# The down projections of a macaron SwiGLU computed by seven block products instead of eight, on one Trainium2 core

## The chip, the core and the metric

The kernel runs on one core of a Trainium2 chip. A core has TensorE (PE in the profile: matrix products, results in eight PSUM banks), VectorE (DVE) and ScalarE (ACT) for elementwise work, GpSimd (POOL), and a queue of transfers that SyncE (SP) issues. The metric is device microseconds (us) of one execution, median over runs. Before the change it is 2217.27 us (three runs, 2216.33 to 2218.95).

## What is computed

Two layers over 512 positions of width 1024. Each is

```
x = x + 0.5 * swiglu(rms_norm(x, ffn1_norm), ffn1_w_gate, ffn1_w_up, ffn1_w_down)
x = x + mix(rms_norm(x, mix_norm))              # two convolutions and a sparse attention, one output projection
x = x + cross_attention(rms_norm(x, xa_norm), rms_norm(mem, mem_norm))
x = x + 0.5 * swiglu(rms_norm(x, ffn2_norm), ffn2_w_gate, ffn2_w_up, ffn2_w_down)

swiglu(h, wg, wu, wd) = (silu(h @ wg) * (h @ wu)) @ wd        # 1024 -> 2816 -> 1024, float32
```

There are so four SwiGLU blocks, called FFN 1 to 4 here. The change is inside them.

## The kernel before

Everything is kept transposed: a chunk is 128 channels on the partitions by 512 positions. x has 8 chunks, the hidden layer 22. A product in float32 is made of three faster ones (`mm3`): each operand is split into a high part, which ACT rounds off (`whi`, or a slot `s`), and a low part, which DVE gets by subtraction (`wlo`), and hi\*hi, hi\*lo and lo\*hi are summed in PSUM. The split of every weight tile therefore costs one ACT and one DVE instruction, and needs one of NW = 4 buffers each for `whi` and `wlo`, which come free when PE has read them. Weights arrive in four staging buffers `stg` of 128x1024.

An FFN goes through the hidden layer in three parts (PARTS: 8, 8 and 6 chunks). In each part it first makes the hidden chunks (gate and up), then adds the part's share of the down product to x.

Gate and up: the first four hidden chunks (PLAIN) by ordinary products of 512 columns, the rest by a scheme with seven block products (Winograd's form of Strassen's). A pair of output chunks times a pair of position halves is a 2x2 block product; instead of eight half-sized products per 2x2 block it takes seven, named A to G, each of 128x128 weights by 256 positions, nf/2 steps j deep. For that, `load_sevens` forms four sums of weight quarters on DVE, and `sevens` forms four sums of input halves, once per FFN. `seven` sends the products to three PSUM banks: A is copied out by ACT, B is added to it by DVE, and so on; the last product G follows behind the A of the next call (the list `late`), since its bank has to be read first.

Down: ordinary products. For each of the 8 output chunks, nf steps of three 512-column matmuls, then one DVE instruction that adds half of the sum to x. In the last part each finished chunk of x is prepared for the next stage (`Norm.chunk`: a square on ACT, a POOL addition, a split on ACT and DVE).

What sets the order: all instructions are recorded first (`Plan.record`), given a cost (`price`) and due time, and then put in order for each engine by a list scheduler (`order`) that has the number of buffers and 62 slots (NSLOT) of 128x512. Each engine then works strictly in that order. The source line of every recorded operation is the same in the profile (L353), so groups are told apart by tile names.

Of the kernel before, what the change touches and what calls it, by code (L numbers as in the profile page):

```python
# [16 lines left out]
P = 128  # L17
# [56 lines left out]
def _quarters(c0, c1):  # L74
    return [(k, DC // 2, m, P, 2) for c in range(c0, c1, 2 * P) for m in (c, c + P) for k in range(2)]
# [95 lines left out]
class Plan:  # L171
# [30 lines left out]
    def record(self, eng, name, args, kw):  # L202
        op = Op()
        op.n, op.eng, op.name, op.args, op.kw, op.succ, op.est, op.floor = (
            len(self.ops), eng, name, args, kw, [], 0.0, self.floor)
        outs = [v for v in (args[0] if args else None, kw.get("out"), kw.get("accum_out")) if isinstance(v, View)]
        ins = [v for v in (*args[1:], *(v for k, v in kw.items() if k not in ("out", "accum_out")))
               if isinstance(v, View)]
        self.price(op, ins, outs)
        op.lat = self.SEEN[eng]  # L210
        deps = set()
# [24 lines left out]
        self.ops.append(op)  # L236

    def price(self, op, ins, outs):
# [27 lines left out]
    def order(self):  # L266
# [40 lines left out]
        while len(done) < len(self.ops):  # L307
# [15 lines left out]
            if op.name == "dma_start":  # L323
                bus = max(bus, t + 1.7) + op.way
                op.end = bus + 0.9
                lanes = lanes[1:] + [op.end + 1.0]
            else:
                op.end = t + cost
# [28 lines left out]
def trunk_kernel(ctx: ExitStack, tc: tile.TileContext, a: dict, out: bass.AP):  # L357
# [169 lines left out]
    def half_quarters(w, c0, m):  # L527
# [3 lines left out]
        for b0, bk, bc, bn, step in BLOCKS[name]:  # L531
            if step == 2 and b0 == 0 and bc == c0 + m * P:
# [3 lines left out]
    def load_sevens(w, c0):  # L536


        H = T
        top, low, s23, s4 = (planned(wpool, g, 1024, F32) for g in ("stg", "stg", "sum", "sum"))  # L540
        nc.sync.dma_start(top, half_quarters(w, c0, 0))
        nc.sync.dma_start(low, half_quarters(w, c0, 1))
        s4 = s4[:, :H]
        nc.vector.tensor_sub(s23[:, H:], top[:, :H], low[:, :H])
        nc.vector.tensor_add(low[:, :H], low[:, :H], low[:, H:])
        nc.vector.tensor_sub(s23[:, :H], low[:, :H], top[:, :H])
        nc.vector.tensor_sub(s4, top[:, H:], s23[:, :H])
        r = {}
        for t, names in ((top, "AB"), (low, "EG"), (s23, "FD"), (s4, "C")):
            hl = split(t, *(planned(wpool, g, 1024, F32R)[:, :t.shape[-1]] for g in ("whi", "wlo")))  # L550
            for i, name in enumerate(names):
                r[name] = [tuple(x[:, i * H + j * P:i * H + (j + 1) * P] for x in hl) for j in range(4)]
        return r

    def load_cols(w, c0, n=256, k0=0, nk=DC):
        return [load(w, k0, nk, c, min(P, c0 + n - c)) for c in range(c0, c0 + n, P)]

# [7 lines left out]
    def sevens(norm):  # L565


        H = T // 2
        r = {name: [] for name in "ABCDEFG"}
        first = None  # L570
        for j in range(DC // 2):
            xe, xo = slot(), slot()
            for i, x in enumerate((xe, xo)):
                c = 2 * j + i
                nc.vector.scalar_tensor_tensor(x, X[c], pcol(norm.gain, norm.i * DC + c), norm.rb, op0=ALU.mult,
                                               op1=ALU.mult)
            t12, t34 = slot(), slot()
            nc.vector.tensor_sub(t12[:, :H], xe[:, H:], xe[:, :H])
            nc.vector.tensor_sub(t12[:, H:], xo[:, H:], t12[:, :H])
            nc.vector.tensor_sub(t34[:, :H], xo[:, H:], xe[:, H:])  # L580
            nc.vector.tensor_sub(t34[:, H:], xo[:, :H], t12[:, H:])
            if j % 2 == 0:
                first = slot(F32R), slot(F32R)
            x = slice(j % 2 * H, (j % 2 + 1) * H)
            r["A"].append(split(xe[:, :H], first[0][:, x], first[1][:, x]))
            for t, names in ((xo, "BC"), (t12, "EF"), (t34, "DG")):
                hl = split(t)
                for i, name in enumerate(names):
                    r[name].append(tuple(y[:, i * H:(i + 1) * H] for y in hl))
        return r  # L590

    def ffn(l, which, norm, nxt, begin=None, end=None):
        wg, wu, wd = ((f"{which}_w_{n}", l) for n in ("gate", "up", "down"))
        H = T // 2
        late = []

        def seven(w, c0, x):


            ws = load_sevens(w, c0)  # L600
            u, v, q = (bank()[:, :H] for _ in range(3))
            o = slot(), slot()
            one, two = slot(), slot()

            def product(acc, name, start, stop):
                for j in range(DC // 2):
                    mm3(acc, ws[name][j], x[name][j], start and j == 0, stop and j == DC // 2 - 1,
                        skip_group_check=True)

            product(u, "A", True, True)  # L610
# [3 lines left out]
            product(v, "E", True, True)  # L614
            nc.scalar.activation(two[:, :H], v, AF.Copy)
            product(q, "B", True, True)
            nc.vector.tensor_add(o[0][:, :H], q, one[:, :H])
            product(u, "F", False, True)
            nc.scalar.activation(one[:, H:], u, AF.Copy)
            product(v, "C", False, True)  # L620
            nc.vector.tensor_add(o[0][:, H:], v, one[:, H:])
            product(u, "D", False, True)
            nc.vector.tensor_add(o[1][:, H:], u, two[:, :H])
            late.append(lambda: product(u, "G", False, True))
            return o, u

        for f0, nf in PARTS:
            hid = []
            last = f0 + nf == FC

            def gated(pg, pu):
# [6 lines left out]
                hid.append(split(g))  # L638

            def gated_sevens(g, u):  # L640
                (ga, gb), gq = g
                (ua, ub), uq = u
                for x in (slice(0, H), slice(H, T)):
                    nc.scalar.activation(ga[:, x], ga[:, x], AF.Silu)
                nc.vector.tensor_mul(ua, ua, ga)
                hid.append(split(ua))
                nc.scalar.activation(gb[:, H:], gb[:, H:], AF.Silu)
                nc.scalar.activation(gb[:, :H], gq, AF.Silu)
                nc.vector.tensor_mul(ub[:, H:], ub[:, H:], gb[:, H:])
                nc.vector.tensor_mul(ub[:, :H], uq, gb[:, :H])  # L650
                hid.append(split(ub))

            if begin and f0 == 0:
                begin(wg, wu)
                norm.finish()
                x7 = sevens(norm)
                for ob in opening:
                    gated(*ob)
            for b in range(1 if begin and f0 == 0 else 0, nf // 2):
                c0 = (f0 + 2 * b) * P  # L660
                if f0 == 0 and b < PLAIN:
                    wgt = load_cols(wg, c0)
                    wut = load_cols(wu, c0)
                    for i in range(2):
# [4 lines left out]
                        if b == 0 and i == 0:  # L669
                            norm.finish()  # L670
                            x7 = sevens(norm)
                        gated(pg, pu)
                else:
                    pair = [seven(w, c0, x7) for w in (wg, wu)]
                    late.append(lambda pair=pair: gated_sevens(*pair))
            while late:
                late.pop(0)()
            for mp in range(DC // 2):
                ws = load_cols(wd, mp * 256, 256, f0, nf)
                halves = end and last and mp == DC // 2 - 1  # L680
                for x in (slice(0, T // 2), slice(T // 2, T)) if halves else (slice(0, T),):
                    for i in range(2):
                        m = 2 * mp + i
                        o = bank()[:, x]
                        for k in range(nf):
                            mm3(o, part(ws[i], k), tuple(t[:, x] for t in hid[k]), k == 0, k == nf - 1)
                        nc.vector.scalar_tensor_tensor(X[m][:, x], o, 0.5, X[m][:, x], op0=ALU.mult, op1=ALU.add)
                        if last:
                            nxt.chunk(m, x)
                        if halves and x.start and i == 0:  # L690
                            end(0)
                if halves:
                    end(1)
# [46 lines left out]
    def mem_part(c):  # L740
        t = slot()
        nc.sync.dma_start(t, a["mem"][:, c * T:(c + 1) * T])
        return t
# [508 lines left out]
```

## Time and profile before

| | |
|---|---|
| median of three runs | 2217.27 us |
| the profiled execution, and its span | 2217.13 us, 2215.3 us |
| PE, DVE, ACT, POOL busy | 2183.5, 1675.1, 1063.5, 153.1 us |
| matmuls | 12922 |
| DMA, mean | 104 GB/s |
| granted TensorE clock, mean | 0.994 of full |

The span is what the profile covers; 1.8 us of the execution lie around it. PE's busy time is modelled, so a share near 100% says that PE always had a matmul under way, not that no faster order exists. Durations of neighbouring DVE instructions overlap a little, and the busy time of an engine counts an overlap once. A row of busy times by stretch reads: start:end, length, then busy us (instructions) of PE, its weight loads, DVE, ACT and POOL, then the granted clock's share, the DMA share and GB/s. A row in order of time reads: start us, duration us, engine, line, operation, output from inputs, shape, count, and in brackets the idle time before it and what ended it.

### The profile page before, as it was taken

To read this page: it belongs to the slowest core of one execution; us is meant where nothing else is said; L and a number is where in the kernel's file an instruction comes from. 1 tells how busy PE (TensorE), PEld (TensorE's weight loads), DVE (VectorE), ACT (ScalarE), POOL (GpSimd) and SP (SyncE) were. 2 spreads that over 40 slices of the span, in tenths; PEclk is the share of its full clock that TensorE was granted. 3 is DMA by queue.
4 is the path that set the end of the run, shared out by engine and by line. 5 is a ranking of instruction groups with operands and counts; after the bars stand their busy time and mean duration, and the time that the engine had idled before them with its cause. 6 is when DMAs were issued, how large, how long until landed. Compare 5 with 4: busy or idle time off the path is not lost. (4 is left out here: it accounts for less than half of the span.)

```text
span 2215.3 us, 32854 instructions
## 1 busy us (share of the span) xinstructions
PE 2183.5 (99%) x12922; PEld 1928.6 (87%) x12922; DVE 1675.1 (76%) x2748; ACT 1063.5 (48%) x1772; POOL 153.1 (7%) x111
## 2 busy tenths in 40 slices
PE   8999999998999999999999999999999999999998
PEld 7989897887788888999989998978787888989897
DVE  8958578999965496766687685779998556958585
ACT  5536255325944353544544453532377344525353
POOL 3000002101020200000100000020100102000001
PEclk9999999999999999999999999999999999999999
DMA  6333333445332223343324333343543313233322
GB/s 216 99 92 113 97 88 110 127 113 145 97 113 67 84 80 113 87 124 86 108 84 121 89 111 90 101 135 89 142 126 104 96 44 99 86 98 113 114 80 74
DMA packets 83755, 230.09 MB, mean 104 GB/s; under 512 B 9616, under 2 KB 23056, under 8 KB 83600
## 3 DMA queue, kind: packets, MB, share of 16 engines
q1 hardware_dynamic: 83600, 228.00, 35.5%
q8 instruction: 101, 1.65, 0.3%
q14 instruction: 54, 0.44, 0.1%
HBM read 211.70 MB, written 2.10 MB: 97 GB/s over the span
## 5 line engine op out<-in xcount | busy, mean ns | idle before, releaser
L353 PE MATMUL ps<-s,whi 128*128 128x256 f32 (+2 forms) x7608 | 1770.4, 330 | 0.8 <-DVE s L353 0.8
L353 PEld LDWEIGHTS ps<-s,whi 128*128 128x128 f32 (+1 forms) x7608 | 1265.0, 190 | 137.1 <-issue 4.3
L353 PE MATMUL ps<-s,wlo 128*128 128x256 f32 (+2 forms) x3804 | 1176.0, 330 | 0.5 <-DVE wlo L353 0.5
L353 PEld LDWEIGHTS ps<-s,wlo 128*128 128x128 f32 (+1 forms) x3804 | 693.6, 190 | 64.7 <-DVE wlo L353 0.7
L353 ACT ACTIVATE whi<-stg 128x1024 fp32r<-128x1024 f32 (+1 forms) x398 | 413.1, 1042 | 694.1 <-PE ps L353 481.0
L353 DVE TENSOR_TENSOR wlo<-stg,whi 128x1024 fp32r<-128x1024 f32 (+1 forms) x398 | 476.0, 1197 | 102.7 <-ACT whi L353 102.3
L353 DVE TENSOR_TENSOR s<-ps,s 128x256 f32<-128x256 f32 (+2 forms) x372 | 186.0, 506 | 108.6 <-PE ps L353 88.2
L353 ACT ACTIVATE s<-ps 128x256 f32<-128x256 f32 (+4 forms) x444 | 188.0, 444 | 154.5 <-PE ps L353 153.6
L353 POOL TENSOR_TENSOR s<-s,s 128x512 f32<-128x512 f32 (+1 forms) x88 | 136.1, 1548 | 1810.1 <-ACT s L353 1539.6
L353 DVE TENSOR_TENSOR s<-s,s 128x512 fp32r<-128x512 f32 (+4 forms) x406 | 252.9, 647 | 6.3 <-ACT s L353 4.1
L353 ACT ACTIVATE s<-s 128x512 fp32r<-128x512 f32 (+3 forms) x355 | 188.8, 546 | 112.6 <-DVE s L353 77.5
L353 DVE SCALAR_TENSOR_TENSOR x<-ps,x 128x512 f32<-128x512 f32 (+1 forms) x98 | 66.7, 681 | 198.6 <-PE ps L353 198.6
L353 ACT ACTIVATE whi<-sum 128x1024 fp32r<-128x1024 f32 (+1 forms) x144 | 121.3, 842 | 137.7 <-PE ps L353 132.3
L353 PE MATMUL ps<-s,s 128*128 128x512 f32 (+7 forms) x688 | 151.8, 365 | 15.9 <-DVE s L353 14.4
L353 DVE TENSOR_TENSOR wlo<-sum,whi 128x1024 fp32r<-128x1024 f32 (+1 forms) x144 | 137.1, 952 | 12.6 <-ACT whi L353 12.6
L353 PEld LDWEIGHTS ps<-s,s 128*128 128x128 f32 (+1 forms) x688 | 107.2, 182 | 43.4 <-DVE s L353 17.2
L353 DVE SCALAR_TENSOR_TENSOR s<-x,cols,s 128x512 fp32r<-128x512 f32 (+1 forms) x96 | 96.7, 1019 | 13.2 <-ACT s L353 11.5
L353 DVE TENSOR_TENSOR sum<-stg,stg 128x512 f32<-128x512 f32 x144 | 99.2, 689 | 2.2
L353 DVE SCALAR_TENSOR_TENSOR s<-s,cols,s 128x256 fp32r<-128x256 f32 (+23 forms) x144 | 100.4, 737 | 0.3
L353 PE MATMUL ps<-whi,s 128*128 128x512 f32 x256 | 82.3, 395 | 0.0
L353 ACT ACTIVATE s<-s,sm 128x512 f32<-128x512 f32 (+3 forms) x128 | 65.2, 551 | 4.0 <-DVE sm L353 4.0
L353 DVE TENSOR_TENSOR x<-x,ps 128x512 f32<-128x512 f32 x32 | 22.0, 686 | 57.6 <-PE ps L353 57.6
(74 smaller groups left out, 796.5 us busy)
## 6 DMA issues: line engine op xcount, KB each, us to landing
stg<-in_ffn_w_gate SPq DMA_DIRECT2D x86, 512.0 KB, 3.6
stg<-in_ffn_w_up SPq DMA_DIRECT2D x86, 512.0 KB, 3.7
stg<-in_ffn_w_down SPq DMA_DIRECT2D x64, 512.0 KB, 3.7
stg<-in_w_in SPq DMA_DIRECT2D x48, 512.0 KB, 3.6
stg<-in_xa_wkv SPq DMA_DIRECT2D x32, 512.0 KB, 3.9
stg<-in_ffn_w_down SPq DMA_DIRECT2D x32, 384.0 KB, 3.2
s<-s SPq DMA_DIRECT2D x64, 128.0 KB, 2.5
stg<-in_w_out SPq DMA_DIRECT2D x16, 512.0 KB, 3.7
```

What stands on the lines that cost most here:

```text
L353: getattr(getattr(nc, op.eng), op.name)(*map(real, op.args), **{k: real(v) for k, v in op.kw.items()})
```

## The change

Down products are made by the same seven products as gate and up, in all parts but the last part of FFN 4.

- A pair of output chunks takes 7 products of nf/2 steps of three matmuls of 256 columns: 84 for nf = 8 and 63 for nf = 6, in place of 48 and 36 matmuls of 512.
- `load_sevens` now serves down weights too (their DRAM layout becomes quarters). It makes its four sums on DVE, as before; signs differ, and the fourth sum lies in a slot instead of a `sum` buffer.
- The hidden chunks are stored for seven products (`Sevens.add`, which also replaces `sevens` for the normalised input): per pair of hidden chunks four more DVE instructions on halves, and four splits in place of two.
- A pair of down outputs leaves PSUM by three subtractions or additions and four multiply-adds of 256 columns on DVE, in place of two multiply-adds of 512.
- The first gate product set of the next part (`ready`) is issued before the down products of this part, and the first down product set runs its first steps (`ahead`) before the last hidden pair is complete.
- `Plan` gets prices for transfers that POOL would issue, of which there are none, and loads of `mem` are ordered behind a tensor instruction.

```diff
-    BLOCKS[_name + "_w_down"] = [b for f0, nf in PARTS for b in _columns(0, D, f0, nf)]
+    BLOCKS[_name + "_w_down"] = [b for f0, nf in PARTS for b in _quarters(0, D, f0, nf)]
...
+    def load_sevens(w, c0, k0=0, nk=DC):
+        n, H = nk // 2, nk // 2 * P
+        top, low, sums = (planned(wpool, g, 1024, F32)[:, :2 * H] for g in ("stg", "stg", "sum"))
+        nc.sync.dma_start(top, quarters(w, k0, c0))
...
+        four = slot(w=H)
+        nc.vector.tensor_add(sums[:, :H], top[:, :H], low[:, :H])
         nc.vector.tensor_add(low[:, :H], low[:, :H], low[:, H:])
+        nc.vector.tensor_add(sums[:, H:], low[:, :H], top[:, :H])
+        nc.vector.tensor_add(four, top[:, H:], sums[:, H:])
...
+        for t, names in ((top, "AB"), (low, "EG"), (sums, "DF"), (four, "C")):
             hl = split(t, *(planned(wpool, g, 1024, F32R)[:, :t.shape[-1]] for g in ("whi", "wlo")))
...
+    class Sevens:
+        def add(self, xe, xo):
+            H = T // 2
+            t12, t34 = slot(), slot()
+            nc.vector.tensor_sub(t12[:, :H], xe[:, :H], xe[:, H:])
+            nc.vector.scalar_tensor_tensor(t12[:, H:], t12[:, :H], -1.0, xo[:, H:], op0=ALU.mult, op1=ALU.subtract)
+            nc.vector.tensor_sub(t34[:, :H], xo[:, H:], xe[:, H:])
+            nc.vector.scalar_tensor_tensor(t34[:, H:], t12[:, H:], -1.0, xo[:, :H], op0=ALU.mult, op1=ALU.subtract)
...
+            self.parts["A"].append(split(xe[:, :H], *to))
+            for t, names in ((xo, "BC"), (t12, "EF"), (t34, "DG")):
+                both = split(t)
...
+            if ahead:
+                for acc, name in ((u, "A"), (v, "E"), (q, "B")):
+                    product(acc, name, True, range(n - 1))
+                js = range(n - 1, n)
+            product(u, "A", True, js)
...
+            by_sevens = not (end and last)
+            hid, some = (Sevens if by_sevens else Whole)(), []
...
+            if not last:
+                ready = kept(wg, (f0 + nf) * P)
...
+                def three(i, ps, x, op, m=m):
+                    to = X[m + i // 2][:, i % 2 * H:(i % 2 + 1) * H]
+                    nc.vector.tensor_tensor(x, *((ps, x) if op == ALU.add else (x, ps)), op=op)
+                    nc.vector.scalar_tensor_tensor(to, x, 0.5, to, op0=ALU.mult, op1=ALU.add)
+                    if i == 1 and last:
+                        nxt.chunk(m)
...
+                u = seven(load_sevens(wd, m * P, f0, nf), hid, three, m == 0)
+                late.append(lambda u=u, fourth=fourth: fourth(u))
```

DVE, second FFN, from a first down part on. Before: the last hidden splits (`s` from `s`), weight splits (`wlo`), and one instruction per chunk of x.

```order
L353 TENSOR_TENSOR s_8488<-s_8419,s_8467 128x512
L353 TENSOR_TENSOR wlo_8495<-stg_8315,whi_8451 128x1024
L353 TENSOR_TENSOR s_8502<-s_8457,s_8492 128x512
L353 TENSOR_TENSOR wlo_8508<-stg_8350,whi_8481 128x1024
L353 SCALAR_TENSOR_TENSOR x_100<-ps_8453,x_100 128x512
L353 TENSOR_TENSOR wlo_8530<-stg_8444,whi_8522 128x1024
L353 SCALAR_TENSOR_TENSOR x_101<-ps_8512,x_101 128x512
L353 TENSOR_TENSOR wlo_8562<-stg_8485,whi_8554 128x1024
```

After, the same place: the last hidden pair (`s_9249`, `s_9279` are its two chunks), then the first output.

```order
L358 TENSOR_TENSOR sum_9357<-stg_9284,stg_9241 128x512
L358 TENSOR_TENSOR s_9463<-s_9447,s_9453 128x512
L358 TENSOR_TENSOR s_9467<-s_9249 128x256
L358 TENSOR_TENSOR s_9469<-s_9279,s_9249 128x256
L358 SCALAR_TENSOR_TENSOR s_9467<-s_9467,s_9279 128x256
L358 TENSOR_TENSOR s_9472<-s_9279,s_9336 128x512
L358 SCALAR_TENSOR_TENSOR s_9469<-s_9467,s_9279 128x256
L358 TENSOR_TENSOR s_9478<-s_9467,s_9474 128x512
L358 TENSOR_TENSOR s_9451<-ps_9416,s_9451 128x256
L358 TENSOR_TENSOR s_9487<-s_9469,s_9481 128x512
L358 TENSOR_TENSOR s_9493<-ps_9282,s_9290 128x256
L358 SCALAR_TENSOR_TENSOR x_100<-s_9451,x_100 128x256
```

The hidden pair takes four more sums and two more 512-wide splits, and a weight sum of the next down pair stands ahead of them on DVE.

PE at that place, after: `ps_9260` is the gate set made ahead (`ready`), `ps_9396` and `ps_9410` are banks of the first down pair.

```order
L358 MATMUL ps_9260<-s_8736,whi_9269 128x256
L358 MATMUL ps_9396<-s_8500,whi_9345 128x256
L358 MATMUL ps_9260<-s_8783,whi_9269 128x256
L358 MATMUL ps_9396<-s_9063,whi_9345 128x256
L358 MATMUL ps_9260<-s_8736,wlo_9287 128x256
L358 MATMUL ps_9396<-s_8500,wlo_9366 128x256
L358 MATMUL ps_9396<-s_9041,whi_9345 128x256
L358 MATMUL ps_9410<-s_9066,whi_9383 128x256
L358 MATMUL ps_9396<-s_9206,whi_9345 128x256
L358 MATMUL ps_9410<-s_9197,whi_9383 128x256
```

Where one bank ran through its 24 matmuls before, two products of the down pair and the end of the gate set now alternate.

DVE, last part of the second FFN, before: three instructions per output chunk of x.

```order
L353 SCALAR_TENSOR_TENSOR x_103<-ps_10913,x_103 128x512
L353 TENSOR_TENSOR wlo_10960<-stg_10854,whi_10952 128x768
L353 SCALAR_TENSOR_TENSOR s_10970<-x_103,cols,s_10963 128x512
L353 SCALAR_TENSOR_TENSOR x_104<-ps_10946,x_104 128x512
L353 TENSOR_TENSOR wlo_10993<-stg_10874,whi_10985 128x1024
```

After, between the second and the third output pair (`sum` and the 384-wide `wlo` are weight sums' splits; rows with `cols` prepare the next stage):

```order
L358 TENSOR_TENSOR s_12448<-ps_12474,s_12448 128x256
L358 TENSOR_TENSOR wlo_12544<-stg_12351,whi_12528 128x768
L358 TENSOR_TENSOR s_12482<-s_12482,ps_12429 128x256
L358 TENSOR_TENSOR wlo_12565<-sum_12416,whi_12549 128x768
L358 SCALAR_TENSOR_TENSOR s_12578<-x_101,cols,s_12562 128x512
L358 TENSOR_TENSOR s_12448<-ps_12459,s_12448 128x256
L358 SCALAR_TENSOR_TENSOR x_105<-ps_12429,x_105 128x256
L358 SCALAR_TENSOR_TENSOR s_12599<-x_102,cols,s_12575 128x512
L358 TENSOR_TENSOR wlo_12609<-s_12485,whi_12591 128x384
L358 SCALAR_TENSOR_TENSOR x_104<-s_12448,x_104 128x256 x2
```

Preparation of x_101 now stands behind splits of the last pair's weights, and two instructions of 256 columns take the place of one of 512.

## Rows read from the trace of the kernel before

**Rows 1.** The page: busy time, share of the span and instructions by engine.
```profile
PE 2183.5 (99%) x12922; PEld 1928.6 (87%) x12922; DVE 1675.1 (76%) x2748; ACT 1063.5 (48%) x1772; POOL 153.1 (7%) x111
```
**Rows 2.** Busy us by stage of FFN 3 (gate-up and down in turn).
```profile
1112.30:1197.70 85.40, 85.40 (x539) 77.67 (x538) 73.78 (x127) 46.03 (x74) 2.63 (x2) 1.00 0.30 89
1197.70:1241.20 43.50, 43.50 (x198) 36.17 (x197) 22.94 (x29) 9.65 (x10) 0.00 (x0) 1.00 0.37 109
1241.20:1322.20 81.00, 81.00 (x671) 80.77 (x670) 65.28 (x98) 47.48 (x78) 0.00 (x0) 1.00 0.34 98
1322.20:1365.70 43.50, 43.50 (x199) 36.17 (x198) 22.93 (x29) 9.65 (x10) 0.00 (x0) 1.00 0.37 109
1365.70:1426.20 60.50, 60.50 (x501) 60.26 (x500) 46.62 (x71) 34.56 (x58) 0.00 (x0) 1.00 0.29 86
1426.20:1459.10 32.90, 32.90 (x148) 26.96 (x147) 24.27 (x28) 16.85 (x24) 8.28 (x6) 1.00 0.48 135
```
**Rows 3.** DVE in order of time, FFN 3: outputs of two neighbouring down chunks.
```profile
1203.16 0.69 DVE L353 SCALAR_TENSOR_TENSOR x<-ps,x 128x512 f32<-128x512 f32 x1 [1.25 <-PE ps L353]
...
1208.60 0.69 DVE L353 SCALAR_TENSOR_TENSOR x<-ps,x 128x512 f32<-128x512 f32 x1 [3.52 <-PE ps L353]
...
1434.36 0.69 DVE L353 SCALAR_TENSOR_TENSOR x<-ps,x 128x512 f32<-128x512 f32 x1 [1.32 <-PE ps L353]
...
1438.44 0.69 DVE L353 SCALAR_TENSOR_TENSOR x<-ps,x 128x512 f32<-128x512 f32 x1 [0.80 <-PE ps L353]
```
**Rows 4.** DVE in order of time: start us, duration us; neighbours of four widths.
```profile
1259.14 1.22 DVE L353 TENSOR_TENSOR wlo<-stg,whi 128x1024 fp32r<-128x1024 f32 x1
1260.27 0.42 DVE L353 TENSOR_TENSOR s<-ps,s 128x256 f32<-128x256 f32 x1
1260.61 0.68 DVE L353 TENSOR_TENSOR s<-s,s 128x512 fp32r<-128x512 f32 x1
1261.21 1.22 DVE L353 TENSOR_TENSOR wlo<-sum,whi 128x1024 fp32r<-128x1024 f32 x1
...
1264.22 0.68 DVE L353 TENSOR_TENSOR stg<-stg 128x512 f32<-128x512 f32 x1
1264.93 0.69 DVE L353 TENSOR_TENSOR sum<-stg,stg 128x512 f32<-128x512 f32 x1
...
1425.59 0.95 DVE L353 TENSOR_TENSOR wlo<-stg,whi 128x768 fp32r<-128x768 f32 x1
1426.46 0.69 DVE L353 TENSOR_TENSOR s<-s,s 128x512 fp32r<-128x512 f32 x1
```
**Rows 5.** What DVE waited for in FFN 3: us in total, times, longest us.
```profile
DVE x L353 <- PE ps L353: 48.4, 25, 3.6
DVE s L353 <- PE ps L353: 22.9, 20, 2.6
DVE wlo L353 <- ACT whi L353: 13.9, 21, 3.5
DVE s L353 <- ACT s L353: 2.9, 6, 0.7
```
**Rows 6.** Busy us by stretch of FFN 1, columns as in rows 2.
```profile
36.00:105.60 69.60, 68.25 (x445) 62.67 (x445) 68.05 (x124) 42.22 (x71) 1.09 (x1) 0.95 0.28 84
74.00:102.90 28.90, 28.90 (x243) 28.90 (x241) 28.38 (x50) 18.56 (x33) 1.09 (x1) 1.00 0.38 110
105.60:149.00 43.40, 43.40 (x198) 36.07 (x197) 23.03 (x28) 9.76 (x11) 0.00 (x0) 1.00 0.37 110
```
**Rows 7.** DVE and POOL groups and instructions in FFN 3's last down part.
```profile
L353 DVE SCALAR_TENSOR_TENSOR s<-x,cols,s 128x512 fp32r<-128x512 f32 x7 | 9.2, 1320 | 2.7 <-ACT s L353 2.5
...
1439.94 1.28 POOL L353 TENSOR_TENSOR s<-s,s 128x512 f32<-128x512 f32 x1 [2.84 <-ACT s L353]
```

More of the change, by code (lines that the diff above doesn't have):

```diff
@@ L556, in load_cols, with load_quarters @@
         return [load(w, k0, nk, c, min(P, c0 + n - c)) for c in range(c0, c0 + n, P)]
+    def load_quarters(w, c, k0, nk):
+        stg, hi, lo = (planned(wpool, g, 1024, dt)[:, :nk * P]
+                       for g, dt in (("stg", F32), ("whi", F32R), ("wlo", F32R)))
+        nc.sync.dma_start(stg, quarters(w, k0, c))
+        hl = split(stg, hi, lo)
+        n = nk // 2
+        return [tuple(t[:, (k % 2 * n + k // 2) * P:(k % 2 * n + k // 2 + 1) * P] for t in hl) for k in range(nk)]
     def load_rows(w, k0, nk, c0):
@@ L575, in sevens, with __init__, add, normalised @@
+    class Whole:
+        def __init__(self):
+            self.parts = []
+        def add(self, *xs):
+            self.parts += [split(x) for x in xs]
+    def normalised(norm):
+        r = Sevens()
+        for j in range(0, DC, 2):
+            xs = slot(), slot()
+            for c, x in enumerate(xs, j):
                 nc.vector.scalar_tensor_tensor(x, X[c], pcol(norm.gain, norm.i * DC + c), norm.rb, op0=ALU.mult,
                                                op1=ALU.mult)
-            t12, t34 = slot(), slot()
@@ L578, in sevens @@
[L578 to L589, printed above, removed]
+            r.add(*xs)
@@ L594, in ffn, with seven, product @@
         H = T // 2
-        late = []
-        def seven(w, c0, x):
-            ws = load_sevens(w, c0)
+        late, ready = [], None
+        def seven(ws, x, three, ahead=False):
             u, v, q = (bank()[:, :H] for _ in range(3))
-            o = slot(), slot()
             one, two = slot(), slot()
[L605 to L610, printed above, removed]
+            n = len(ws["A"])
+            def product(acc, name, start, js=range(n)):
+                for j in js:
+                    mm3(acc, ws[name][j], x.parts[name][j], start and j == 0, j == n - 1, skip_group_check=True)
+            js = range(n)
+            if ahead:
[3 more added lines that the diff above has]
+            product(u, "A", True, js)
             while late:
@@ L637, in gated @@
                 nc.vector.tensor_mul(g, pu, s)
-                hid.append(split(g))
+                some.append(g)
+                if len(some) == 2:
+                    hid.add(some.pop(0), some.pop(0))
             def gated_sevens(g, u):
@@ L655, in ffn @@
                 norm.finish()
[L656 removed]
+                x7 = normalised(norm)
                 for ob in opening:
@@ L670, in ffn @@
                             norm.finish()
-                            x7 = sevens(norm)
+                            x7 = normalised(norm)
                         gated(pg, pu)
                 else:
-                    pair = [seven(w, c0, x7) for w in (wg, wu)]
+                    pair = [kept(wg, c0) if ready is None else ready, kept(wu, c0)]
+                    ready = None
                     late.append(lambda pair=pair: gated_sevens(*pair))
+            if not last:
+                ready = kept(wg, (f0 + nf) * P)
@@ new lines, in ffn, with fourth @@
+            while late and not (late[1:] == [] and ready):
+                late.pop(0)()
+            for m in range(0, DC, 2):
+                if not by_sevens:
+                    ws = [load_quarters(wd, c * P, f0, nf) for c in (m, m + 1)]
+                    halves = end and last and m == DC - 2
+                    for x in (slice(0, H), slice(H, T)) if halves else (slice(0, T),):
+                        for i in range(2):
+                            o = bank()[:, x]
+                            for k in range(nf):
+                                mm3(o, ws[i][k], tuple(t[:, x] for t in hid.parts[k]), k == 0, k == nf - 1)
+                            nc.vector.scalar_tensor_tensor(X[m + i][:, x], o, 0.5, X[m + i][:, x], op0=ALU.mult,
+                                                           op1=ALU.add)
+                            if last:
+                                nxt.chunk(m + i, x)
+                            if halves and x.start and i == 0:
+                                end(0)
+                    if halves:
+                        end(1)
+                    continue
+                def three(i, ps, x, op, m=m):
[4 more added lines that the diff above has]
+                        nxt.chunk(m)
+                def fourth(u, m=m):
+                    to = X[m + 1][:, :H]
+                    nc.vector.scalar_tensor_tensor(to, u, -0.5, to, op0=ALU.mult, op1=ALU.add)
+                    if last:
+                        nxt.chunk(m + 1)
+                u = seven(load_sevens(wd, m * P, f0, nf), hid, three, m == 0)
+                late.append(lambda u=u, fourth=fourth: fourth(u))
@@ L676, in ffn @@
             while late:
                 late.pop(0)()
[L678 to L693, printed above, removed]
```

92 lines of the change are left out of this document (47 added, 45 removed).

## The prediction

> **What bounds the kernel now.** The page first: PE is busy 99% of the span, DVE 76%, ACT 48% [rows 1]. Averages don't tell what a change in one stage is worth, so next the busy times by stage, for FFN 3, the one with no start or end of the program in it [rows 2]. The six rows are gate-up and down of the three parts in turn. The reader is to see three things: PE is busy for the whole of each; ACT never passes 60%; and DVE is at 73.8 of 85.4, 65.3 of 81.0 and 46.6 of 60.5 us in gate-up, at 22.9 of 43.5 in the long down parts, and at 24.3 of 32.9 in the short one. So PE bounds all stages, and DVE has its room in the down parts, just where the change puts work.
>
> Then the beat of both engines, in order of time. Two outputs of a down part lie 5.44 us apart for 24 matmuls, in the short part 4.08 for 18 [rows 3]: 0.2267 us per matmul of 512 columns. The gate-up of part 3 is six product sets of 84 matmuls, 504 in 60.5 us [rows 2]: 0.1200 us per matmul of 256. Half the columns cost more than half the time. On DVE what counts is start to start, not duration: 0.34 us for 256 columns, 0.60 for 512, 1.13 for 1024 [rows 4], 0.87 for 768; a 512-wide one that needs its predecessor's result starts after 0.71. A 512-wide instruction is shown with 0.68, so some 0.08 us of each lies under the next one.
>
> **The change part by part.** *PE.* A down pair of nf = 8 costs 48 x 0.2267 = 10.88 us before and 84 x 0.1200 = 10.08 after: 0.80 less. With nf = 6 it is 36 x 0.2267 = 8.16 against 63 x 0.1200 = 7.56: 0.60 less. There are 4 pairs in a part, so 3.2, 3.2 and 2.4 us per FFN; the last part of FFN 4 stays as it is. 32 x 0.80 + 12 x 0.60 = 32.8 us, all on the path as long as PE bounds. That is 1.5% at most: one eighth of the products goes, but the beat of the narrower ones gives half of it back.
>
> The Trainium skill ("TensorE: Matmul & The Clock Gate", section Back-to-back issue gap) states N/2.4 + 2.5 ns for a matmul by itself, 215.8 and 109.2 ns here. By it the pairs would save 1.19 and 0.89 us, 48.7 us in all, as an estimate. The rows say 226.7 and 120.0 ns; the sum goes by them.
>
> *DVE, weights.* Per down pair: four sums of 512 columns, 4 x 0.60 = 2.40; the split of the sums, 1.13 + 0.60 = 1.73; outputs, seven of 256 at 0.34 in place of two of 512, 2.38 - 1.20 = 1.18. Together +5.31 us. With nf = 6 the sums have 384 columns, a width that no row shows: between 0.34 and 0.60, and I take the middle, 0.47. Then 1.88 + 0.87 + 0.47 + 1.18 = 4.40 (3.75 and 5.05 by the two ends).
>
> *DVE, hidden chunks.* Per pair four sums of 256 columns and splits of 256 + 3 x 512 instead of 2 x 512: 1.36 + 0.34 + 1.80 - 1.20 = +2.30 us. The normalised input has as many instructions as before.
>
> An FFN gets 8 x 5.31 + 4 x 4.40 + 11 x 2.30 = 85.4 us of DVE work, FFN 4 60.9 (8 down pairs, 8 hidden pairs): 317 us in all, nearly ten times what PE saves. It costs nothing only where DVE was idle.
>
> *The rest.* ACT gets two more splits and three copies per down pair and two more splits per hidden pair; with 164 of 347 us in FFN 3 [rows 2] it keeps cover. Bytes, and the number of weight transfers, stay. Signs, prices of POOL transfers and the later `mem` loads move nothing that is waited for: 0, where a load was hidden under PE and still is. `ready` and `ahead` move work and add none; they let PE run while the last hidden pair is split.
>
> *What of it lies on the path.* A down part cannot start before its hidden pairs, and gate-up cannot run far ahead, since one product set takes all four `whi` and `wlo`. So I add the stages by part, gate-up with its down, for FFN 3 [rows 2]:
>
> - part 1: PE 85.4 + 43.5 - 3.2 = 125.7; DVE 73.8 + 22.9 + 4 x 2.30 + 4 x 5.31 = 127.1
> - part 2: PE 81.0 + 43.5 - 3.2 = 121.3; DVE 65.3 + 22.9 + 9.2 + 21.2 = 118.6
> - part 3: PE 60.5 + 32.9 - 2.4 = 91.0; DVE 46.6 + 24.3 + 6.9 + 17.6 = 95.4
>
> Two corrections. DVE's busy time counts the 0.08 us wherever nothing followed; DVE waited 25 + 20 + 21 + 6 = 72 times [rows 5], and new work closes these gaps: 6 us of the 341, which I share out: 124.8, 116.5, 93.8. (Bounds: nothing, and all 382 instructions, 31 us.) And a full DVE is not quite full: where it was the bound, in FFN 1, it was busy 28.38 of 28.9 us with PE at its full beat [rows 6], and 68.05 of 69.6 over a longer stretch. Divided by 0.98: 127.3, 118.9, 95.7. Of each pair of numbers the larger holds: 127.3, 121.3, 95.7. Before they were 128.9, 124.5 and 93.4. FFN 3: -1.6 - 3.2 + 2.3 = -2.5 us, and FFN 2 the same. FFN 4 keeps its last part: -1.6 - 3.2 = -4.8.
>
> FFN 1 is the one in which DVE bounds already: from 36 us to the first down part at 105.6 [rows 6]. Part 1 from 36 us on: (68.05 + 23.03 + 9.2 + 21.2 - 2.3) / 0.98 = 121.6, so its end moves from 149.0 to 157.6, +8.6; part 2 has 2.4 us of room on DVE and takes some 2 back. With -3.2 and +2.3 for the others: +5.7.
>
> Sum: 5.7 - 2.5 - 2.5 - 4.8 = -4.1 us. The profiled execution took 2217.13 us (span 2215.3), the median is 0.14 above it. Forecast 2213 us: nearly all of the 32.8 us is given back, because DVE becomes a second bound.
>
> **The rivals.** *DVE finds the time* (18%). If every instruction's 0.08 us is hidden once DVE is full, an FFN's 341 us become 310 and PE bounds everything but the short down parts, which DVE alone must hold: 24.3 + 17.6 less 72 x 0.08 is 36 us against PE's 30.5, 5.5 us in three FFNs. 2217 - 32.8 + 16.5 = 2201. For it speaks the stretch of 28.9 us; against it that a split waits for ACT 21 times and an output for PE 45 times per FFN [rows 5], which more work does not abolish.
>
> *Outputs read too late* (22%, slower). Product G of a set reuses the bank that DVE must read after D, and only A of the next set lies between: 12 x 0.12 = 1.44 us, 1.08 with nf = 6. One weight split ahead of the read in DVE's queue makes 1.13 + 0.42 = 1.55 us, and PE stands. With DVE 81% full in gate-up that is rare; at 97% it need not be. There are 72 + 44 = 116 sets. If each loses 0.3 us on average, +35: 2248. From 0.07 us per set on (8.5 us) the kernel is slower than before. Against it: in the full stretch of FFN 1 PE kept 28.9 us / 0.12 = 241 matmuls, and 243 overlap it [rows 6]; but that is three sets. The preparation of x in the short part adds to this side: its splits took 1.32 us while POOL added for 1.28 [rows 7], 0.6 over a 512-wide beat.
>
> *Slots run out* (8%, slower). The split input takes 28 of the 62 slots, a part's hidden chunks 28 instead of 16. Six are left, while a set wants five and the gate set made ahead keeps two more. If each end of a long part costs two products of 1.44 us, 8 x 2.9 = +23: 2236. For it speaks that PE's order at the first down part alternates between banks, as if steps came singly.
>
> *DVE drains* (2%). If an instruction held DVE for its whole duration, 0.08 us on each of 580 (382 + 12 x 11 + 11 x 6) would be added where it now overlaps, about 40 us per FFN: some 380 us against 347 before, or +130, 2347. Start to start 0.60 for 0.68 speaks against it [rows 4]. It is the rule of the Trainium skill ("VectorE: DVE Perf Modes", section The DRAIN you can't avoid: the next operation does not start until the pipe empties); the trace does not agree where neighbours are independent, and comes near it where one needs the other (0.71).
>
> **How the numbers follow.** The forecast has 50%. Its own range: without the 6 us correction 14 us more in all, 2227; with a fill of 1.00 instead of 0.98, 13 less, 2200; the width of 384 moves 3 x 4 x 0.65 = 8 us within it. What this kernel's measurement can tell from no change is about 0.2%, 4.4 us: 2212.8 to 2221.7. Of the forecast's 50, 24 lie below, 18 within and 8 above. With 18 for the first rival below and 32 for the others above: faster 0.42, same 0.18, slower 0.40. The range for eight in ten leaves out the far half of the first rival and the far ends of the slow ones: 2197 to 2246. It leans to neither side much, since two engines with 338 and 341 us of work in each FFN make the outcome hang on a few per cent of fill.
>
> **What would show it.** In the changed profile: down sets at 84 x 0.12 us (if the matmul beat were another, the PE term falls); DVE busy about 1675 + 317 - 24 = 1968 us, 89%; FFN 3's parts near 127, 121 and 96 us; part 1 of FFN 1 ending near 158 us; the short down parts longer than 33 us with PE waiting for DVE there; the granted clock still near 1. The forecast is wrong if PE shows no waits for DVE in the short parts (first rival), if PE waits for an `s<-ps` of DVE once per set (second), or if ACT or DVE wait for PE to free slots at the ends of parts (third).

## The result

The changed kernel takes 2242.31 us (median of 4 runs, 2241.65 to 2244.77), the kernel before 2216.8 beside it: a ratio of 1.0115, 95% interval 1.0103 to 1.0127. It is slower by 25.5 us where 4 less were forecast; the time lies inside the stated range of 2197 to 2246, on the side that had a chance of 0.40. The profiled execution took 2244.77 us, the longest of the four; its span is 2243.0 us.

The page after, busy time by engine, answers to [rows 1]; under it the granted TensorE clock in 40 equal slices, in tenths.

```profile
PE 2180.6 (97%) x14398; PEld 1993.1 (89%) x14398; DVE 1971.6 (88%) x3478; ACT 1213.8 (54%) x2038; POOL 162.7 (7%) x111
...
PEclk9989999999999999999999999999989999999999
```

DVE's 1971.6 us are the 1968 forecast. PE is less busy by 3 us only, where 32.8 less were forecast: the mean clock fell from 0.994 to 0.982, so part of its work ran slower.

FFN 3 by its three parts, against [rows 2] (each part's gate-up and down together; the first two ends lie where the part's last output is read):

```profile
1128.10:1272.90 144.80, 138.92 (x963) 130.14 (x963) 137.16 (x236) 77.94 (x122) 5.30 (x3) 0.98 0.33 97
1272.90:1394.10 121.20, 121.20 (x1010) 121.17 (x1009) 115.24 (x193) 71.40 (x113) 0.00 (x0) 1.00 0.36 105
1394.10:1482.40 88.30, 85.10 (x671) 82.72 (x670) 84.82 (x148) 55.66 (x94) 8.13 (x5) 0.98 0.32 92
```

The first row holds a gate set of 10.08 us that belongs to the second part, the second hands one on to the third. Corrected for that the parts took 134.7, 121.2 and 98.4 us, against 128.3, 124.5 and 94.0 before by the same reading. Where a part ends in seven products PE has by its end also done 1.8 us of the next part's work (the last part of FFN 4, unchanged, came out 1.9 us shorter). The tables count that back: they take 1.8 us off a first part and add them to a last part.

The whole program by the same ends, changed minus before, in us, and what the prediction had:

| | FFN 1 first | FFN 2-4 first | middle parts (4) | last parts, FFN 1-3 | two mixing stages | sum |
|---|---|---|---|---|---|---|
| forecast | +8.6 | -4.8 | -14.8 | +6.9 | 0 | -4.1 |
| measured | +3.1 | +12.5 | -13.0 | +15.6 | +9.6 | +27.7 |

The middle parts of FFN 2 to 4 came as forecast, -3.2 us each; FFN 1's gave 3.4 where 5.2 were forecast. First parts, last parts and the stages between the FFNs are not right. Where the first part of FFN 3 loses: windows of 2 us as gate-up goes over into down (columns as in rows 2), then PE's waits there, then DVE at the end of them.

```profile
1222.00:1224.00 2.00, 2.00 (x19) 2.00 (x18) 2.00 (x4) 0.33 (x1) 0.00 (x0) 1.00 0.28 39
1224.00:1226.00 2.00, 1.31 (x11) 1.11 (x11) 2.00 (x5) 1.02 (x2) 0.00 (x0) 1.00 0.63 223
1226.00:1228.00 2.00, 0.97 (x9) 0.77 (x7) 1.91 (x5) 0.63 (x1) 0.00 (x0) 1.00 0.00 0
1228.00:1230.00 2.00, 0.45 (x3) 0.46 (x4) 2.00 (x6) 0.71 (x2) 0.00 (x0) 1.00 0.00 0
1230.00:1232.00 2.00, 1.50 (x7) 1.00 (x5) 2.00 (x6) 0.82 (x2) 0.00 (x0) 0.63 0.04 8
1232.00:1234.00 2.00, 1.83 (x8) 1.83 (x9) 2.00 (x6) 1.81 (x5) 0.00 (x0) 0.50 0.34 43
1234.00:1236.00 2.00, 2.00 (x12) 2.00 (x11) 0.50 (x1) 0.22 (x1) 0.00 (x0) 0.50 0.58 219
1236.00:1238.00 2.00, 2.00 (x13) 2.00 (x13) 1.13 (x1) 1.37 (x3) 0.00 (x0) 0.66 0.00 0
1238.00:1240.00 2.00, 2.00 (x19) 2.00 (x18) 1.10 (x2) 1.86 (x2) 0.00 (x0) 1.00 0.41 68
```

```profile
1225.28 0.39 PE L358 MATMUL ps<-s,whi 128*128 128x256 f32 x1 [0.69 <-DVE s L358]
1229.55 0.50 PE L358 MATMUL ps<-s,whi 128*128 128x256 f32 x2 [2.57 <-DVE s L358]
1230.48 0.57 PE L358 MATMUL ps<-s,whi 128*128 128x256 f32 x1 [0.20 <-DVE s L358]
1232.17 0.80 PE L358 MATMUL ps<-s,whi 128*128 128x256 f32 x2 [0.47 <-ACT s L358]
```

```profile
1228.80 0.69 DVE L358 TENSOR_TENSOR s<-s,s 128x512 fp32r<-128x512 f32 x1
1229.40 0.42 DVE L358 SCALAR_TENSOR_TENSOR s<-s,s 128x256 f32<-128x256 f32 x1
...
1233.80 0.69 DVE L358 TENSOR_TENSOR wlo<-s,whi 128x512 fp32r<-128x512 f32 x1
1236.87 1.22 DVE L358 TENSOR_TENSOR wlo<-stg,whi 128x1024 fp32r<-128x1024 f32 x1 [2.37 <-ACT whi L358]
```

PE waits 3.9 us at the last hidden pair, 3.5 of them for DVE's splits and 0.5 for an ACT instruction behind them, while DVE works with hardly a gap; once the splits are done DVE itself idles 2.37 us. So its room comes right behind the place that needed it. After the wait PE runs at 1.2 GHz for some 6.8 us (the four windows' missing shares of the clock, 0.37 + 0.50 + 0.50 + 0.34, make 3.4 us, and at half speed that is twice as long), 12 or 13 matmuls in 2 us instead of 19: 3.4 us more. With the saving, -3.2 + 3.9 + 3.4 = +4.1; measured +4.6 (134.7 - 128.3 - 1.8).

### The profile page after: what moved, and what is told of

It reads as the page before. It is cut to its first block, busy times and chain, and to the rows that moved or that the text cites. A ratio compares the mean times of both kernels' runs of the same rounds, so it can differ in the third digit from the quotient of the medians.

```text
span 2243.0 us, 36866 instructions
## 1 busy us (share of the span) xinstructions
PE 2180.6 (97%) x14398; PEld 1993.1 (89%) x14398; DVE 1971.6 (88%) x3478; ACT 1213.8 (54%) x2038; POOL 162.7 (7%) x111
## 5 line engine op out<-in xcount | busy, mean ns | idle before, releaser
L358 PEld LDWEIGHTS ps<-s,whi 128*128 128x128 f32 (+1 forms) x8592 | 1369.7, 192 | 113.1 <-DVE s L358 26.8
L358 PE MATMUL ps<-s,wlo 128*128 128x256 f32 (+1 forms) x4296 | 1223.4, 309 | 8.6 <-DVE wlo L358 8.6
L358 PEld LDWEIGHTS ps<-s,wlo 128*128 128x128 f32 x4296 | 783.9, 192 | 49.3 <-DVE wlo L358 11.1
L358 ACT ACTIVATE s<-ps 128x256 f32<-128x256 f32 (+5 forms) x576 | 239.0, 431 | 196.7 <-PE ps L358 190.0
L358 DVE TENSOR_TENSOR s<-s,s 128x512 fp32r<-128x512 f32 (+4 forms) x497 | 303.4, 634 | 17.6 <-ACT s L358 13.9
L358 DVE TENSOR_TENSOR sum<-stg,stg 128x512 f32<-128x512 f32 (+1 forms) x232 | 157.3, 678 | 0.4
L358 ACT ACTIVATE whi<-s 128x512 fp32r<-128x512 f32 (+1 forms) x116 | 72.0, 620 | 114.9 <-PE ps L358 113.3
L358 DVE SCALAR_TENSOR_TENSOR s<-s,cols,s 128x511 f32<-128x511 f32 (+15 forms) x144 | 103.8, 768 | 0.4
L358 DVE TENSOR_TENSOR wlo<-s,whi 128x512 fp32r<-128x512 f32 (+1 forms) x116 | 79.9, 689 | 3.3 <-ACT whi L358 1.9
L358 DVE TENSOR_TENSOR stg<-stg 128x512 f32<-128x512 f32 (+1 forms) x116 | 79.5, 685 | 0.4
```

What stands on the lines that cost most here:

```text
L358: getattr(getattr(nc, op.eng), op.name)(*map(real, op.args), **{k: real(v) for k, v in op.kw.items()})
```

## The experiments

Theory D: DVE is in debt when the first part's gate-up ends. Theory M: the late `mem` loads cost time in the mixing stages. Rivals: S (slots), L (any new order disturbs the unchanged stages), C (POOL and DVE slow each other). This is where each kernel's time stands against the kernel before, in us by the ends used above (with sixty slots a part has by its end done 1.0 us more of the next part's work, eight matmuls, which is counted back too):

| kernel | FFN 1 first | FFN 2-4 first | middle | last, FFN 1-3 | mixing |
|---|---|---|---|---|---|
| changed | +3.1 | +12.5 | -13.0 | +15.6 | +9.6 |
| middle parts only | -5.2 | +0.2 | -13.3 | 0.0 | +12.6 |
| middle and last | -5.2 | +0.3 | -12.8 | +15.3 | +11.0 |
| no input sums | -3.7 | -9.5 | -12.8 | +15.0 | +9.8 |
| filler | +2.1 | +7.7 | -13.2 | +15.3 | +10.0 |
| before, `mem` late | -5.2 | 0.0 | 0.0 | 0.0 | +13.1 |
| middle only, `mem` earlier | -5.5 | +0.7 | -13.3 | +2.9 | +1.1 |
| changed, `mem` earlier | +3.2 | +9.3 | -13.0 | +18.1 | -3.2 |
| sixty slots | +4.1 | +14.5 | -7.8 | +15.2 | +10.1 |
| POOL relief | +4.1 | +13.0 | -12.7 | +18.5 | -4.6 |
| no set ahead | +4.3 | +19.6 | +3.8 | +15.5 | +7.7 |

**Which parts cost.**

```diff
-            by_sevens = not (end and last)
+            by_sevens = f0 == 8          # second run: f0 > 0 and not (end and last)
```

> Seven products for down in the middle part of each FFN alone, plain products in the first and the last part (and no gate set ahead of a plain part). Theory D (DVE in debt): the loss lies where the first part goes from gate-up to down, because DVE is full through all of that gate-up and its debt has to be paid before the first down product; the middle parts gave 3.2 us each in the changed kernel, so 2217 - 4 x 3.2 = 2204 us. Rival S (slots run out): the same 2204, since a long part with seven products stays and showed no wait. Rival L (the order or the clock of the unchanged mixing stages is disturbed by any change): 2210 to 2220, since 9.6 us of the loss were measured in the two mixing stages.

2211.32 us, ratio 0.9979 (0.9970 to 0.9988). In these two runs a part with plain down products makes no gate set ahead either. The middle parts give 13.3 us, as D and S say, but the mixing stages still lose 12.6, which is L's point.

> Seven products in the middle and the last part, plain ones in the first part. The last parts cost 4.3, 1.5 and 4.3 us in the changed kernel, and the mixing stages behind two of them 5.6 and 4.0. D: 10 us over the kernel with the middle part alone, 2214, and 2224 if the mixing stages' loss comes from the last part's late end. L: mixing stages lose whether or not the last part is changed, so no more than 10 us lie between this kernel and the one with the middle part alone.

2223.82 us, ratio 1.0036 (1.0023 to 1.0048): 12.5 over the run above (14.3 between the two profiled executions): 15.3 more in the last parts, 1.6 less in the mixing stages. These lose nearly alike with and without, so the last part's late end is not their cause. (The expectation's 4.3, 1.5 and 4.3 us for the last parts leave out the 1.8 us that the tables count back.)

**The debt.**

```diff
-            r.add(*xs)
+            r.add(*xs, sums=False)      # in normalised: t12, t34 = xe, xo, no sums
```

> The changed kernel, with the four sums of halves of the normalised input left out (16 DVE instructions of 256 columns per FFN, 16 x 0.34 = 5.4 us of DVE work in the first part's gate-up; the later products use unsummed halves, so part of the computation is changed). D: the debt of some 4 us is gone, with it PE's wait and the fall of the clock behind it, 7 to 8 us in each of four FFNs: 2242 - 30 = 2212. S: slots come free as before, the wait at the first down product stays: 2240. If only the wait and not the dip goes: 2227.

2216.61 us (ratio 1.0002, 0.9993 to 1.0011), 26 under the changed kernel, 5 above D's 2212. The first parts of FFN 2 to 4 go from +12.5 to -9.5, the full 3.2 us each: 5.4 us less on DVE took 7.3 off each part, wait and fall of the clock. The same place in FFN 3:

```profile
1195.00:1215.00 20.00, 20.00 (x168) 19.97 (x167) 20.00 (x34) 12.39 (x21) 0.00 (x0) 1.00 0.33 91
1215.00:1235.00 20.00, 20.00 (x169) 20.00 (x169) 18.67 (x33) 10.33 (x16) 0.00 (x0) 1.00 0.40 122
```

168 and 169 matmuls in 20 us is the full beat, at full clock. D holds for FFN 2 to 4; in FFN 1 PE still waits there for 2.7 us. (The edit also saves two slots per input pair, but those were in use at the start of gate-up, far ahead of the wait.)

**The clock.**

```diff
+                    for _ in range(32):
+                        nc.tensor.matmul(spare, ones_r, x7.parts["A"][0][0], start=True, stop=True)
```

> The changed kernel with 32 needless matmuls of 256 columns (3.84 us) on PE at the place where it waits for DVE at the first down product of each FFN. If the granted clock falls because PE idles there, PE stays at 2.4 GHz and some 3.4 us per FFN come back: 2242 - 13 = 2229. If the clock falls for another reason, or the fillers stand beside the wait and not in it: 2242 to 2242 + 4 x 3.84 = 2257.

2238.16 us (ratio 1.0097, 1.0081 to 1.0112), 4 less than the changed kernel where 13 less were expected: the expectation had the clock's gain without the fillers' own time. FFN 3 at the same place:

```profile
1228.00:1230.00 2.00, 1.70 (x15) 1.49 (x14) 1.90 (x5) 1.01 (x3) 0.00 (x0) 1.00 0.00 0
1230.00:1232.00 2.00, 1.65 (x12) 1.44 (x13) 2.00 (x6) 0.86 (x3) 0.00 (x0) 1.00 0.00 0
1232.00:1234.00 2.00, 1.55 (x10) 1.35 (x11) 2.00 (x3) 1.69 (x3) 0.00 (x0) 1.00 0.72 225
```

The clock stays at 2.4 GHz here: it had fallen because PE idled. The fillers' 3.84 us and 1.1 us of waits that remain are 1.0 more than the wait they replace; less 3.4 of slow clock that is -2.4, and the part came out 2.2 shorter.

**The mixing stages.**

```diff
+        nc.behind = next(op for op in reversed(nc.ops) if op.eng == "tensor")   # in mem_part, kernel before
         nc.sync.dma_start(t, a["mem"][:, c * T:(c + 1) * T])
+        nc.behind = None
```

> The kernel before, with one edit of the change alone: loads of mem wait for the tensor instruction recorded last before them. Theory M: this edit moves mem's preparation (squares, products with the norm, splits) out of the first FFN, where DVE bounds, into the mixing stages, where DVE is full too; with the middle part alone the first part of FFN 1 ended 5.2 us earlier than before, mixing 1 took 8.4 and mixing 2 4.3 us longer. So 2216 + 8.4 + 4.3 - 5.2 = 2223.5. Rival L (any other order does it, not this edit): 2216, or mixing stages that lose without FFN 1 gaining. My prediction priced this edit at 0.

2224.85 us, ratio 1.0038 (1.0026 to 1.0051): this one edit costs 8.1 us. Products of `mem` with its norm, in the kernel before and in this one (ns min/median/max, first and last start):

```profile
L353 DVE TENSOR_TENSOR s<-s,mrb x16: 409/414/418, 370.0 to 380.2; 128x256 f32<-128x256 f32 x16
```

```profile
L353 DVE TENSOR_TENSOR s<-s,mrb x16: 411/418/421, 521.1 to 1624.4; 128x256 f32<-128x256 f32 x16
```

Before, those of both layers were done at the start of the first mixing stage; now each layer's come in the midst of its own. In the first mixing stage, before and with the edit, by the same ends:

```profile
366.50:616.30 249.80, 239.01 (x1201) 195.41 (x1200) 238.91 (x500) 133.80 (x264) 23.52 (x14) 0.98 0.42 118
```

```profile
361.00:619.30 258.30, 246.79 (x1211) 199.87 (x1209) 237.25 (x492) 131.60 (x259) 27.36 (x19) 0.97 0.42 119
```

DVE has no more work than before, but it comes later: 8.5 us more. The granted shares of the two rows, 0.98 and 0.97, say that some 3 of them are the slower clock (an estimate: 0.02 x 249.8 against 0.03 x 258.3 us); which work holds PE up in the rest was not taken apart. FFN 1 gains 5.2 by having no `mem` in its start. M holds, and L falls: the rest of the program is within 0.2 us.

```diff
-        nc.behind = next(op for op in reversed(nc.ops) if op.eng == "tensor")
+        nc.behind = nc.mark             # set where an FFN's last part begins
```

> Seven products in the middle parts alone, and mem loads that wait for the last tensor instruction ahead of each FFN's last part instead of the last one ahead of their place. M: mem's preparation can use the last part, where the plain down product leaves DVE room, so the mixing stages come back to about 398 us each: 2211 - 12 = 2200. If the first part of FFN 1 does not keep its 5.2 us: 2205. L: 2211 still.

2203.43 us, ratio 0.9937 (0.9925 to 0.9950): with seven products in the middle parts alone, the fastest here. The mixing stages come back but for 1.1 us, FFN 1 keeps its gain, and the last parts pay 2.9.

> The changed kernel with the same earlier loads of mem. M: mixing 1 and 2 took 5.6 and 4.0 us more than before, and DVE has less room in a last part by seven products, so between nothing and all of it comes back: 2233 to 2242. D stays as it is: PE waits at the first down product of each FFN as before.

2230.5 us, ratio 1.006 (1.0044 to 1.0075): 12 us come back: 12.8 in the mixing stages and 3.2 in the first parts of FFN 2 to 4, which still lose 9.3, while the last parts lose 2.5 more. The change with no such wait of the `mem` loads at all was not tried.

**Slots.**

```diff
-NSLOT = 62
+NSLOT = 60
```

> The changed kernel with 60 slots instead of 62. S (slots decide the wait at the first down products): two slots less hold up more of the work ahead, 2 products of 1.44 us or more in each of 4 first parts, 2254 or above. D: DVE's work decides, slots don't: 2242, within 4 us.

2252.55 us, ratio 1.0159 (1.0145 to 1.0173): 10 us more than with 62, near S's 2254 and beyond D's 2242. Slots are scarce. Half of the loss is in the middle parts; the first parts of FFN 2 to 4 take 2.1 us more in all. In FFN 2 PE waits there with 62 slots, then with 60:

```profile
877.91 0.50 PE L358 MATMUL ps<-s,whi 128*128 128x256 f32 x2 [2.80 <-DVE s L358]
```

```profile
870.93 0.86 PE L358 MATMUL ps<-s,whi 128*128 128x256 f32 x5 [1.08 <-ACT whi L358]
...
880.52 0.50 PE L358 MATMUL ps<-s,whi 128*128 128x256 f32 x2 [1.28 <-DVE s L358]
...
883.93 0.50 PE L358 MATMUL ps<-s,whi 128*128 128x256 f32 x2 [1.96 <-DVE s L358]
```

With two slots less PE waits longer, but the clock is slow there for 3.4 us instead of 6.8, which hides the difference in FFN 2. At 62 slots taking work from DVE was enough to end the wait; whether more slots would shorten it was not tried, so S is not excluded as a part of it.

**Can POOL take the debt?**

```diff
-            nc.vector.tensor_sub(t12[:, :H], xe[:, :H], xe[:, H:])      # of the input, and one of t34's
+            eng.tensor_sub(t12[:, :H], xe[:, :H], xe[:, H:])            # eng = nc.gpsimd
-                nc.vector.tensor_mul(s, s, norm.rb)
+                nc.gpsimd.tensor_mul(s, s, norm.rb)
```

> The changed kernel with the earlier loads of mem (2230.5 us), and DVE work of the first part given to POOL, which stands idle there: two of the four sums of halves of the normalised input (8 x 0.34 us per FFN) and one 512-wide product in each of the four hidden chunks made by plain products (4 x 0.60), together 5.1 us. D: as with the 5.4 us left out, 7 us per first part come back: 2230.5 - 28 = 2203. Rival C (POOL and DVE slow each other: beside POOL's addition a 512-wide DVE instruction took 1.32 us where it takes 0.75 without): POOL's 15 us per FFN cost DVE up to 10, more than they save: 2235 to 2250.

> The same, with the last part of each FFN by plain products. The last parts cost 4.3, 1.5 and 4.3 us against plain ones: 10 us less than with them, so 2193 by D, and 2225 to 2240 by C.

2236.22 (ratio 1.0092, 1.0078 to 1.0105) and 2226.35 us (1.0047, 1.0033 to 1.0061): C's case. In FFN 3 DVE, POOL and PE in order of time, in the first of the two:

```profile
1147.18 1.23 DVE L358 SCALAR_TENSOR_TENSOR s<-x,cols,s 128x512 f32<-128x512 f32 x1
1148.33 1.78 DVE L358 TENSOR_TENSOR stg<-stg 128x512 f32<-128x512 f32 x1
...
1151.25 0.74 DVE L358 SCALAR_TENSOR_TENSOR s<-x,cols,s 128x512 f32<-128x512 f32 x1
...
1152.24 1.76 DVE L358 TENSOR_TENSOR wlo<-stg,whi 128x1024 fp32r<-128x1024 f32 x1
...
1169.51 1.21 DVE L358 TENSOR_TENSOR wlo<-sum,whi 128x1024 fp32r<-128x1024 f32 x1
1171.90 0.69 DVE L358 TENSOR_TENSOR s<-ps,s 128x512 f32<-128x512 f32 x1 [1.18 <-POOL s L358]
```

```profile
1144.89 4.67 POOL L358 TENSOR_TENSOR s<-s,s 128x256 f32<-128x256 f32 x3
1149.51 1.19 POOL L358 TENSOR_TENSOR s<-s 128x256 f32<-128x256 f32 x1
1152.07 0.85 POOL L358 TENSOR_TENSOR s<-s,s 128x256 f32<-128x256 f32 x1 [1.36 <-DVE s L358]
...
1161.83 10.04 POOL L358 TENSOR_TENSOR s<-s,s 128x512 f32<-128x512 f32 x1 [5.89 <-ACT s L358]
```

```profile
1175.38 0.87 PE L358 MATMUL ps<-s,whi 128*128 128x256 f32 x4 [3.40 <-ACT s L358]
```

Beside POOL's sums DVE instructions are longer: 1.23 against 0.74, 1.78 against 0.68, 1.76 against 1.22. A 512-wide product on POOL took 10.04 us while DVE was full, and PE waited 3.40 for the split behind it. The wait moved from the end of gate-up to its start. This fits what the Trainium skill says ("SBUF — State Buffer", section SBUF: two separate sides): a DVE instruction with two SBUF inputs and a GpSimd instruction that reads SBUF take turns at a shared port pair, one blocking the other for a whole instruction. Ten microseconds are more than one such turn. The trace shows when they ended: DVE ran without a gap until 1170.72, then stood idle for 1.18 us because it needed POOL's product itself, and POOL was done. It was so in all four FFNs (9.49, 10.04, 10.04 and 10.05 us, each ending in such a gap of DVE). POOL got through only once DVE had run dry; why it lost every turn before, no run here shows.

> The changed kernel with the earlier loads of mem (2230.5 us), and of POOL's relief only the two sums of halves of the normalised input (8 of 256 columns per FFN, 2.7 us of DVE work), none of the 512-wide products, of which one took 10.04 us on POOL and held PE up for 3.4. D without contention: half of what 5.4 us less gave, 4 x 3.7 us: 2216. C (the eight sums take 1.2 us each on POOL, and DVE instructions beside them were 0.4 to 1.1 us longer): DVE gains nothing, 2228 to 2234.

2233.39 us, ratio 1.0076 (1.0059 to 1.0093), C again: without the wide products there is no gain either (2230.5 with the earlier `mem` loads alone).

**The set ahead.**

```diff
-            if not last:
+            if False:
                 ready = kept(wg, (f0 + nf) * P)
```

> The changed kernel without the gate product set that is made ahead of each down part. D: PE has 10.08 us less to do while DVE pays its debt, DVE has 7.8 us less to do before the first down product (2.40 of sums, 4.0 of splits, 1.36 of outputs), so the wait in each first part grows by 2.3 us and the clock falls longer: 2250 to 2260. S (the set's slots are what is missing at the end of a part): the waits shrink, 2230 to 2240.

2268.12 us, ratio 1.0237 (1.0223 to 1.0251), 26 over the changed kernel and beyond D's 2260: not the first parts alone lose (7 us in FFN 2 to 4), the middle parts lose 17. So the gate set covers a wait in the middle parts too; that it is the same wait, for the splits of the last hidden pair, is argued.

## Why the prediction was wrong

That the time lies inside the range speaks for no mechanism: the slow side of the range stood for rivals with other causes.

- *The PE term held.* 3.2 us per long part, shown four times over in the middle parts, and in the first parts once DVE had less to do.
- *The DVE term held.* 1971.6 us busy, 1968 forecast.
- **The step that failed: "So I add the stages by part, gate-up with its down".** DVE's room in a down part can't pay for what gate-up needs before it. Alone, the first part's gate-up had 73.8 + 9.2 of 85.4 us, and the gate set ahead and the first down pair's weights stood in front of the down as well; the room came 10 us too late (PE first waits at 1224.6, DVE first idles at 1234.5). By the sum the first part of FFN 3 should have taken 127.3 us, DVE's, 1.6 over PE's 125.7; it took 132.9 (134.7 - 1.8), with 3.9 us of PE's waits and 3.4 of slow clock in it. In the middle parts, where no input is prepared, the sum was good. The two lists of the order ahead of the prediction showed it: a weight sum of the next pair and six hidden instructions on DVE just ahead of the first output.
- *The clock was left out.* "The granted clock still near 1" was wrong: 3.4 us in each first part of FFN 2 to 4 come from it, about as much as the wait, and 6.8 in FFN 1's (next row). Over the program the mean of 0.982 against 0.994 stands for some 27 us (an estimate: 0.018 x 2243.0 less 0.006 x 2215.3), as much as the whole loss.

```profile
114.40:128.10 13.70, 9.55 (x39) 8.66 (x40) 11.96 (x25) 7.08 (x13) 0.00 (x0) 0.50 0.13 38
```

A last part can have it too. PE's wait there in FFN 2, with no fall of the clock, then in FFN 3 with the window behind it:

```profile
1120.55 0.39 PE L358 MATMUL ps<-s,wlo 128*128 128x256 f32 x1 [1.27 <-DVE wlo L358]
```

```profile
1468.95 0.39 PE L358 MATMUL ps<-s,wlo 128*128 128x256 f32 x1 [2.04 <-DVE wlo L358]
...
1470.00:1475.00 5.00, 5.00 (x33) 5.00 (x33) 4.58 (x8) 2.67 (x6) 1.73 (x1) 0.71 0.34 98
```

- *The last parts* were forecast at +2.3 each; FFN 1's to 3's took +6.1, +3.3 and +6.2. The same step failed. FFN 3's last part in two halves, then the second half of FFN 1's:

```profile
1394.10:1440.00 45.90, 45.90 (x384) 45.88 (x383) 43.49 (x77) 28.01 (x46) 0.00 (x0) 1.00 0.30 87
1440.00:1482.40 42.40, 39.20 (x290) 36.85 (x289) 41.33 (x72) 27.65 (x48) 8.13 (x5) 0.96 0.35 97
```

```profile
330.00:372.30 42.30, 38.58 (x294) 36.07 (x293) 41.64 (x73) 27.73 (x49) 8.01 (x5) 1.00 0.38 105
```

PE bounds the first half, where DVE has 2.4 us to spare, and DVE the second, where PE idles for 3.2: neither engine's room serves the other. POOL's additions also stretch some of DVE's weight splits there, which I had seen [rows 7] and given to a rival, not to the sum:

```profile
1463.78 1.73 DVE L358 TENSOR_TENSOR wlo<-stg,whi 128x768 fp32r<-128x768 f32 x1
...
1466.88 2.02 DVE L358 TENSOR_TENSOR wlo<-stg,whi 128x768 fp32r<-128x768 f32 x1
...
1462.99 5.09 POOL L358 TENSOR_TENSOR s<-s,s 128x512 f32<-128x512 f32 x3 [324.22 <-ACT s L358]
```

These splits took 0.95 before [rows 4]. Why FFN 2's last part cost 3 us less than the others stays open. It is not the clock: FFN 1's last part kept the full clock, and without the input sums FFN 3's did too (granted clock 1.00) and took +5.7. Nor is it the splits: none of 768 columns took over 0.96 us in FFN 1's.
- *The later `mem` loads* were priced at 0 because their transfers are hidden. What moved was the DVE and ACT work behind them: +8.1 us by themselves in the kernel before, about a third of the loss.
- *FFN 1's first part* was forecast at +8.6 and took +3.1; the `mem` edit alone gives -5.2 there, so seven products cost some 8.3. That this is near 8.6 is in part luck: the 6.8 us of slow clock in it were not in the forecast.
- *The rivals.* "Outputs read too late" gave nearly the right time (2248) by the wrong mechanism: the middle parts keep the full beat. "Slots run out" had the place and nearly the price (2236); at 62 slots less work on DVE was enough to end the wait, so slots alone are not the cause. "DVE finds the time" and "DVE drains" fell.

## What to carry to other kernels

Balance engines up to each point where one must wait for the other, not over a stage with slack at its end: room behind a dependency pays nothing ahead of it. Price every wait of PE that a change adds at the wait plus the slow clock that may follow. An edit that only holds back a transfer also holds back everything computed from it; ask where that work will land.

## What the runs showed that I had not expected

- After 3.9 us of waits, broken by a few matmuls, PE ran at 1.2 GHz for some 6.8 us; after a wait of 1.27 us in FFN 2's last part it did not slow, after one of 2.04 us in FFN 3's it ran slow for about 3 (0.71 over 5 us). With needless matmuls in the wait of FFN 3's first part it kept 2.4 GHz.
- A 512-wide fp32 multiplication on POOL took 10.04 us beside a full DVE, against 1.28 for an addition of that size in [rows 7], and it ended only when DVE stopped to wait for it.
